# Moving a layer's activation tiles by some bytes in SBUF, and splitting its 512-column feed-forward products into 256-column ones

## The chip, the cores and the metric

The kernel runs on one core of one Trainium2 chip. TensorE multiplies 128x128 blocks into PSUM, VectorE (DVE) and ScalarE (ACT) work on SBUF and PSUM, GpSimd (POOL) and SyncE (SP) issue DMAs. The metric is the device time of one execution in microseconds; the time before is the median of three runs. SBUF has 128 partitions, and every tile begins at the same byte in each of them. That byte, modulo 256, is what this document calls a tile's start.

## The reference

One decoder layer on x of 256 tokens by 2048 channels, in float32:

```python
for l in range(DEPTH):                                  # DEPTH = 1
    mod = jax.nn.silu(c) @ w_ada[l] + b_ada[l]
    sh1, sc1, g1, sh2, sc2, g2 = jnp.split(mod[:, None, :], 6, axis=-1)
    h = x * (1.0 + sc1) + sh1
    y = token_mixer(h, ...)          # w_in, two mixers, two projections, w_out
    x = layer_norm(DEEPNORM_ALPHA * x + g1 * y, ln1_g[l], ln1_b[l])
    h = x * (1.0 + sc2) + sh2
    gate, up = jnp.split(h @ w_ffn_in[l], 2, axis=-1)   # 2048 x 11264
    y = (jax.nn.silu(gate) * up) @ w_ffn_out[l]         # 5632 x 2048
    x = layer_norm(DEEPNORM_ALPHA * x + g2 * y, ln2_g[l], ln2_b[l])
```

The token mixer projects h to queries, keys, values and gates, runs causal attention with 8 heads and a gated delta rule with 16 heads, projects both back to 2048 channels, merges them by sigmoid gates and projects once more.

## The kernel before, in words

**Products in parts.** TensorE multiplies in the fp32r type. To keep float32's accuracy each operand is split into a high part (rounded to fp32r) and a low part (the rest), and a product of two matrices is made of three: high by high, high by low, low by high. `split_w` (lines 221 and 222) splits every weight block of 128x1024 elements, the high part by an ACT copy and the low part by a DVE subtraction. `load_w` brings the block from HBM by a DMA on SP's queue; five raw blocks, four high and four low ones are held.

**Two ways to put a block through TensorE.** In `ws_mm` (lines 304 to 306) the weight is the stationary operand, 128x128 at a time, and the activations move: each product streams 256 columns, the 256 tokens, into one half of a PSUM bank. A block holds 4 contraction tiles by 2 output tiles, so it takes 8 times 3, or 24 products. Lines 304, 305 and 306 are high weight by high activation, high by low, low by high. Almost all of the input projection, the sigmoid gates and both projections back run this way. In `xs_unit` (lines 352 to 354) the activations are stationary and the weights move, 512 columns at a time: the attention's values, the delta rule's z, the output projection and the feed-forward output.

**The feed-forward input** has a third way, `ws_wide` (lines 309 to 316). There the high and the low part of an activation tile lie side by side in `h2`, so that one product of 512 columns (line 311) does high by high and high by low at once, into the two halves of a whole bank; after eight of these come eight products of 256 columns for the low weights (line 315), into the first half. That is 16 products a block. A unit is 256 columns of `w_ffn_in`, four blocks, and takes two banks of the four that `mm()` gives. When a unit is done, `summed` (lines 1222 to 1227) adds the two halves of each bank: an ACT copy and a DVE addition for each of two banks. Then come Silu for a gate unit, and for an up unit the product with the gate and the split for the next stage. The first two gate and two up units (line 1246 on) are made with `ws_mm` while the norm before them ends; the other 20 pairs, 40 units or 160 blocks, with `wide_unit`.

**Order of the work.** `step` and `run` put all blocks of the layer in one list; weights are loaded and split up to three blocks ahead. `tick` after each block lets side jobs advance: the delta rule and the attention, which are chains over DVE, ACT, PE and DMA (lanes "pre", "main", "moba"), and the sums over `w_ada` (line 241). Before the first weight blocks the kernel makes the first part of `mod`, and during the first 290 us it keeps loading 1 MB pieces of `w_ada` into the tiles of `ring`.

**Where the tiles lie.** A pool gives its tiles addresses in the order of their first use, after 4,096 bytes of scratch and four small constants. In bytes modulo 256 the tiles start as follows in the program before:

| tile | used as | start before |
|---|---|---|
| s0, s1 (h high, low; later the two halves of h2) | moving in lines 304 to 306, 311, 315; stationary in lines 352 to 354 for values and z | 128 |
| ya (attention's output) | moving | 128 |
| ybA, ybBh (delta rule's output) | moving | 64 |
| ybBl (delta rule's output, low, second half) | moving | 96 |
| weight blocks hi, lo | stationary in lines 304 to 315, moving in lines 352 to 354 | 64 |
| mh, ml, ach, acl | stationary in lines 352 to 354 | 64 |

Inside a tile every operand begins a multiple of 512 bytes further on.

Of the kernel before, what the change touches and what calls it, by code (L numbers as in the profile page):

```python
# [10 lines left out]
F32 = mybir.dt.float32  # L11
F32R = mybir.dt.float32r
AF = mybir.ActivationFunctionType
OP = mybir.AluOpType
# [4 lines left out]
P = 128  # L19
D = 2048  # L20
S = 256
KT = D // P
DFF = 5632
# [69 lines left out]
def layer(ctx, tc, a, out):  # L93
    nc = tc.nc
    v_, s_, g_, t_, dma = nc.vector, nc.scalar, nc.gpsimd, nc.tensor, nc.sync
    sdma = nc.gpsimd

    perm = ctx.enter_context(tc.tile_pool(name="perm", bufs=1))
# [10 lines left out]
    k1 = p1.enter_context(tc.tile_pool(name="p1", bufs=1))  # L109

    def e2(nm, shape):
        return k1.tile(shape, F32, tag="e2", name=nm, bufs=3)

    x_sb = perm.tile([P, KT, S], F32, tag="s2", name="x_sb")
    xv = a["x"][0].rearrange("(h p) d -> p h d", p=P)
    cols = perm.tile([P, V_END], F32, name="cols")
# [56 lines left out]
    def rest(n=1):  # L173
        return -n
# [52 lines left out]
    def split(hi, lo, src, scale=None):  # L227
        if scale is None:
            s_.copy(hi, src)
            v_.tensor_tensor(lo, src, hi.bitcast(F32), op=OP.subtract)  # L230
        else:
            s_.activation(hi, src, AF.Copy, scale=scale)
            v_.scalar_tensor_tensor(lo, src, scale, hi.bitcast(F32), op0=OP.mult, op1=OP.subtract)
# [39 lines left out]
    def mm():  # L273
        return pm.tile([P, 512], F32, tag="mm", name="mm")
# [3 lines left out]
    def step(w, k0, kn, c0, cn, post, begun=0, pin=False):  # L278
        prog.append((lambda: split_w(load_w(w, k0, kn, c0, cn), kn, cn, pin), post, begun))
# [25 lines left out]
                t_.matmul(o, hi[:, i, c], al, start=False, stop=False)  # L305
                t_.matmul(o, lo[:, i, c], ah, start=False, stop=(last and i == kn - 1 and t == 1))  # L306

    def ws_wide(box, both, hi, lo, k0, kn, first, last):
        for i in range(kn):
            for t in range(2):  # L310
                t_.matmul(box[t].rearrange("p (u i) -> p u i", u=2), hi[:, i, t * P:(t + 1) * P], both[k0 + i],  # L311
                          start=(first and i == 0), stop=False)
        for i in range(kn):
            for t in range(2):
                t_.matmul(box[t][:, :S], lo[:, i, t * P:(t + 1) * P], both[k0 + i][:, 0, :], start=False,  # L315
                          stop=(last and i == kn - 1))

    def pairs_of(ps):
        return ps.rearrange("p (t i) -> p t i", t=2)
# [85 lines left out]
    def g8(slot, nm, shape, dt=F32):  # L405
        return k1.tile(shape, dt, tag=f"g{slot}", name=nm)
# [9 lines left out]
    def load_ba():  # L416
# [1 line left out]

    kqs = [g8(2 * b, f"kq{b}", [P, 8, S]) for b in range(2)]
    vts = [g8(2 * b + 1, f"v{b}", [P, 8, S]) for b in range(2)]  # L420
    ring = [k1.tile([P, 2, 2048], F32, tag="ma0", name="r0"), k1.tile([P, 1, 2048], F32, tag="ma1", name="r1"),
            k1.tile([P, 1, 2048], F32, tag="g4", name="r2")]
    spare = ring[1][:, 0, :]
    ring = [t[:, i, :] for t in ring for i in range(t.shape[1])]
    jobs = []
# [121 lines left out]
    btd = dr.tile([VH, S], F32, name="btd")  # L547

    def gates_ba():
        w6 = k1.tile([P, 6, 2, VH], F32, name="w6")  # L550
        x, m, e, q, y, z = [w6[:, i] for i in range(6)]

        def heads(i):
            return dtb[:, i:i + 1, :].to_broadcast([P, 2, VH])

        tri = e2("tri", [P, 2, P])
        sdma.dma_start(tri, a["cst"][:, C_TRI:].rearrange("p (u i) -> p u i", u=2))
        ps = pg.tile([P, 2, 32], F32, tag="gd", name="ps_g")
        for i in range(2):
            t_.matmul(ps[:, i, :], ba[:, i * P:(i + 1) * P], cst[:, C_BA:C_BA + 32], start=True, stop=True)  # L560
        s_.activation(e, ps[:, :, 0:16], AF.Exp, scale=-1.0)
        v_.tensor_scalar(e, e, 1.0, None, op0=OP.add)
        v_.reciprocal(bcs[:, 3:5, :], e)
        v_.tensor_tensor(x, ps[:, :, 16:32], heads(0), op=OP.add)
        v_.tensor_scalar(m, x, -1.0, None, op0=OP.mult)
        v_.tensor_tensor(m, m, x, op=OP.max)
        s_.activation(e, m, AF.Exp, scale=-1.0)
        s_.activation(z, heads(1), AF.Exp)
        v_.tensor_scalar(q, e, 2.0, None, op0=OP.add)
        v_.reciprocal(q, q)  # L570
        v_.tensor_tensor(e, e, q, op=OP.mult)
        v_.tensor_tensor(q, e, e, op=OP.mult)
        v_.tensor_scalar(m, q, 1.0 / 15, None, op0=OP.mult)
        yield 1.2
        for n in (13, 11, 9, 7, 5, 3):
            v_.scalar_tensor_tensor(m, m, 1.0 / n, q, op0=OP.add, op1=OP.mult)
        v_.scalar_tensor_tensor(m, m, 1.0, e, op0=OP.add, op1=OP.mult)
        v_.tensor_scalar(x, x, 0.0, None, op0=OP.max)
        v_.scalar_tensor_tensor(x, m, 2.0, x, op0=OP.mult, op1=OP.add)
        v_.scalar_tensor_tensor(y, x, -1.0, z, op0=OP.mult, op1=OP.mult)  # L580
        yield 1.0
        yield rest()
        ps = pg.tile([P, 3, VH], F32, tag="gd", name="ps_c")
        t_.matmul(ps[:, 0:2, :], tri[:, 0, :], y, start=True, stop=True)
        t_.matmul(ps[:, 2, :], tri[:, 1, :], y[:, 0, :], start=True, stop=True)
        v_.tensor_copy(bcs[:, 0:3, :], ps)
        yield rest()
        tp = pt.tile([P, P], F32, tag="tp", name="tp")
        t_.transpose(tp[:80], bcs.rearrange("p u h -> p (u h)"), ident)
        rw = e2("gr", [80, P])  # L590
        s_.copy(rw, tp[:80])
        for i in range(2):
            c = slice(i * P, (i + 1) * P)
            sdma.dma_start(gcd[:, c], rw[16 * i:16 * i + 16])
            sdma.dma_start(btd[:, c], rw[48 + 16 * i:64 + 16 * i])
        yield 0.1
# [34 lines left out]
    def bc_heads(t, h0):  # L631
        return bass.AP(tensor=t.tensor, offset=t.offset + h0 * S, ap=[[0, P], [S, 2], [1, S]])

    kqn = [k1.tile([P, 3, 16], F32, name=f"kqn{b}") for b in range(2)]

    def squares(b, t0):
        ss = pg.tile([P, 512], F32, tag="gd", name="ss")
# [309 lines left out]
    cur = {}  # L947
# [80 lines left out]
    for j in range(8):  # L1028
        ws_unit(h_ops, w_in, O_GB + 256 * j, KT,
                lambda ps, j=j: s_.activation(cur["sgb"][:, 2 * j:2 * j + 2, :], ps, AF.Sigmoid))  # L1030
# [53 lines left out]
    def resid(ps, c0, cn, gb, base, dst, st, n):  # L1084
        cc = slice(c0, c0 + cn)
        for h in range(2):
            t = (cur["k3"].tile([P, 512], F32, tag="up", name="rt", bufs=2) if "k3" in cur
                 else e2("rt", [P, 512]))[:, :cn]
            v_.tensor_tensor(t, ps[h], gb[:, cc], op=OP.mult)
            v_.scalar_tensor_tensor(dst[:, h, cc], base[:, h, :], ALPHA, t, op0=OP.mult, op1=OP.add)  # L1090
            v_.bn_stats(st[:, h, n, :], dst[:, h, cc])
# [13 lines left out]
    def load_sqrt():  # L1105
        tc.keep_in_program_order(s_.activation(sm[:, 0, 0:1], epsc[:, 0:1], AF.Sqrt))

    sa = perm.tile([P, 2, KT], F32, name="sa")

    def mod2():  # L1110
        drain("ada")
        v_.tensor_scalar(sa[:, 0, :], adac[:, 64:80], 1.0, None, op0=OP.add)
        v_.tensor_tensor(sa[:, 1, :], sa[:, 0, :], cols[:, 112:128], op=OP.mult)
        v_.tensor_tensor(sa[:, 1, :], sa[:, 1, :], adac[:, 48:64], op=OP.add)
        v_.tensor_tensor(sa[:, 0, :], sa[:, 0, :], cols[:, 96:112], op=OP.mult)
        load_sqrt()
# [47 lines left out]
    h2_ops, act_ops = [[], []], [[], []]  # L1164
    pss, h2 = [], []
# [46 lines left out]
    def k3_tile(nm):  # L1212
        return cur["k3"].tile([P, 2, S], F32, tag=nm, name=nm, bufs=2)
# [5 lines left out]
        v_.tensor_tensor(sg, psu, sg, op=OP.mult)  # L1219
        split(ach[:, 2 * j:2 * j + 2, :], acl[:, 2 * j:2 * j + 2, :], sg)  # L1220

    def summed(box, nm):
        t = k3_tile(nm)
        for n in range(2):
            s_.copy(t[:, n, :], box[n][:, S:])
            v_.tensor_tensor(t[:, n, :], t[:, n, :], box[n][:, :S], op=OP.add)
        return t

    def wide_unit(c0, fin):
        box = []  # L1230
        for k in range(0, KT, 4):
            def post(hi, lo, k=k):
                if k == 0:
                    box.extend([mm(), mm()])
                ws_wide(box, h2, hi, lo, k, 4, k == 0, k == KT - 4)
                if k == KT - 4:
                    fin(box)
                tick()

            step(w_fi, k, 4, c0, 256, post)  # L1240
# [47 lines left out]
    do(ffn_more)  # L1288

    def ffn_unit(j):  # L1290
        def gate(box):
            sg = cur["sgw"] = summed(box, "sg")
            s_.activation(sg, sg, AF.Silu)

        def up(box):
            ach, acl = cur["act"]
            t = summed(box, "up")
            v_.tensor_tensor(t, t, cur["sgw"], op=OP.mult)
            split(ach[:, 2 * j:2 * j + 2, :], acl[:, 2 * j:2 * j + 2, :], t)

        wide_unit(256 * j, gate)
        wide_unit(DFF + 256 * j, up)

    for j in range(2, DFF // 256):
        ffn_unit(j)
# [76 lines left out]
    for n, (c0, cn) in enumerate(ln_blocks()):  # L1382
# [6 lines left out]
        def fin(ps, n=n, c0=c0, cn=cn):  # L1389
            cc = slice(c0, c0 + cn)  # L1390
            r = cur["r"]
            resid(ps, c0, cn, cur["g2b"], r[:, :, cc], r, cur["st"], n)
            for h in range(2):
                v_.tensor_tensor(r[:, h, cc], r[:, h, cc], cur["g"][:, cc], op=OP.mult)
# [41 lines left out]
```

## Time and profile before

| | us |
|---|---|
| median of 3 runs | 1731.93 |
| lowest, highest | 1727.89, 1731.94 |
| profiled execution, its own time | 1724.92 |
| span of its core | 1723.2 |
| PE busy | 1674.6 (97%) |
| DVE busy | 1232.4 (72%) |
| ACT busy | 819.3 (48%) |
| feed-forward input, wide part | 1028 to 1469 |

PE's granted clock was 1.00 of full speed in nearly all windows. Matmuls overlap: a product of 256 columns is shown as 0.28 us long, but the next one starts 0.11 to 0.12 us after it. So the price of a product is read from the distance between starts, in the timeline, and not from the mean of one. In the timeline, products of one line that follow each other directly are merged to one row with their count.

### The profile page before, as it was taken

What the parts mean: (1) busy time and instruction counts of PE and PEld (TensorE: products, weight loads), DVE (VectorE), ACT (ScalarE), POOL (GpSimd) and SP (SyncE); (2) the same over time, 40 slices, a digit from 0 to 9 for tenths busy, and PEclk for the clock granted to TensorE, in tenths of its full rate; (3) what the DMA queues carried; (4) which work ended last, traced back from release to release, by engine and by line L of the source; (5) the groups of instructions that cost most, each with busy time, mean ns of one, the idle gap of its engine ahead of it and who ended that gap; (6) DMA issues with size and microseconds to landing.
All of it is one profiled execution on the core that took longest, in us unless ns stands there. A gap on an engine that the chain in (4) does not pass through costs nothing.

```text
span 1723.2 us, 28196 instructions
## 1 busy us (share of the span) xinstructions
PE 1674.6 (97%) x11129; PEld 1518.9 (88%) x11129; DVE 1232.4 (72%) x1775; ACT 819.3 (48%) x1134; POOL 39.5 (2%) x61
## 2 busy tenths in 40 slices
PE   6999999999999998999989999999999999999998
PEld 4898999889999777999978998888888888888898
DVE  6899987899755796567986787666666655455454
ACT  3544445868545445464334454444444444433342
POOL 0000010110100001000000000000000000000000
PEclk9999999999999999999999999999999999999999
DMA  9999996665777668678998468777777756755652
GB/s 365 335 363 348 338 328 218 186 205 167 244 235 231 209 214 266 218 225 262 306 347 288 159 206 271 240 237 241 231 246 231 241 190 194 236 196 183 202 189 98
DMA packets 114296, 417.43 MB, mean 242 GB/s; under 512 B 13406, under 2 KB 14414, under 8 KB 108656
## 3 DMA queue, kind: packets, MB, share of 16 engines
q1 hardware_dynamic: 109652, 400.12, 69.3%
q0 software_dynamic: 4512, 15.51, 3.3%
q8 instruction: 87, 1.43, 0.3%
q14 instruction: 45, 0.37, 0.1%
HBM read 408.14 MB, written 7.44 MB: 241 GB/s over the span
## 4 chain that ended last, share of the span: by engine, by line
PE 76%; DVE 8%; issue 7%; DMA 6%; ACT 1%; POOL 0%; SPq 0%; DVEq 0%; ACTq 0%; POOLq 0%
PE mm L311 17%; PE mm L315 9%; PE mm L306 8%; PE mm L304 8%; PE mm L305 8%; PE mm L353 6%; PE mm L354 6%; PE mm L352 6%; DVE lo L222 3%; DMA raw_a<-in_w_ada 2%; DVE r L241 1%; PE ps L757 1%; ACT hi L221 1%; DMA mbd<-ma 1%; PE mm L370 1%
## 5 line engine op out<-in xcount | busy, mean ns | idle before, releaser
L221 ACT CAST hi<-raw 128x1024 fp32r<-128x1024 f32 (+2 forms) x572 | 581.3, 1020 | 769.2 <-PE mm L311 199.1
L222 DVE TENSOR_TENSOR lo<-raw,hi 128x1024 fp32r<-128x1024 f32 (+2 forms) x572 | 672.2, 1185 | 278.1 <-ACT hi L221 275.1
L304 PE MATMUL mm<-s,hi 128*128 128x256 f32 x1184 | 338.1, 286 | 5.3 <-ACT hi L221 5.0
L306 PE MATMUL mm<-s,lo 128*128 128x256 f32 x1184 | 333.0, 282 | 8.1 <-DVE lo L222 7.9
L305 PE MATMUL mm<-s,hi 128*128 128x256 f32 x1184 | 332.5, 281 | 0.0
L311 PE MATMUL mm<-h,hi 128*128 128x512 f32 x1280 | 319.0, 391 | 0.0
L311 PEld LDWEIGHTS mm<-h,hi 128*128 128x128 f32 x1280 | 228.8, 188 | 39.5
L304 PEld LDWEIGHTS mm<-s,hi 128*128 128x128 f32 x1184 | 224.9, 190 | 10.3 <-ACT hi L221 8.0
L306 PEld LDWEIGHTS mm<-s,lo 128*128 128x128 f32 x1184 | 223.6, 189 | 11.2 <-DVE lo L222 10.2
L305 PEld LDWEIGHTS mm<-s,hi 128*128 128x128 f32 x1184 | 224.7, 190 | 0.3
L315 PEld LDWEIGHTS mm<-h,lo 128*128 128x128 f32 x1280 | 171.1, 188 | 13.2
L315 PE MATMUL mm<-h,lo 128*128 128x256 f32 x1280 | 174.1, 278 | 0.0
L353 PE MATMUL mm<-lo,ach 128*128 128x512 f32 (+1 forms) x352 | 127.7, 363 | 0.0
L352 PE MATMUL mm<-hi,ach 128*128 128x512 f32 (+1 forms) x352 | 127.7, 363 | 0.0
L354 PE MATMUL mm<-hi,acl 128*128 128x512 f32 (+1 forms) x352 | 127.6, 363 | 0.0
L241 DVE CUSTOM_DVE_ANT_0 raw_a<-raw_a,cb,cols 128x1024 f32<-128x1024 f32 x56 | 71.9, 1283 | 76.6 <-DMA raw_a<-in_w_ada 76.5
L241 DVE CUSTOM_DVE_ANT_0 raw_a<-raw_a,cb,ada_half 128x1024 f32<-128x1024 f32 x56 | 71.9, 1283 | 62.1 <-DMA raw_a<-in_w_ada 62.1
L241 DVE CUSTOM_DVE_ANT_0 r<-r,cb,cols 128x2048 f32<-128x2048 f32 (+1 forms) x40 | 92.6, 2322 | 8.5 <-DMA r<-in_w_ada 8.4
L353 PE MATMUL mm<-lo,s 128*128 128x512 f32 x192 | 76.7, 399 | 3.2 <-DVE lo L222 3.1
L352 PE MATMUL mm<-hi,s 128*128 128x512 f32 x192 | 77.3, 404 | 0.0
L354 PE MATMUL mm<-hi,s 128*128 128x512 f32 x192 | 75.9, 395 | 0.0
L353 PEld LDWEIGHTS mm<-lo,ach 128*128 128x128 f32 x352 | 66.5, 189 | 10.6 <-DVE lo L222 0.2
(342 smaller groups left out, 2435.7 us busy)
## 6 DMA issues: line engine op xcount, KB each, us to landing
raw<-in_w_ffn_in SPq DMA_DIRECT2D x176, 512.0 KB, 4.4
raw<-in_w_in SPq DMA_DIRECT2D x168, 512.0 KB, 4.6
raw_a<-in_w_ada SPq DMA_DIRECT2D x112, 512.0 KB, 4.5
raw<-in_w_ffn_out SPq DMA_DIRECT2D x88, 512.0 KB, 4.0
r<-in_w_ada SPq DMA_DIRECT2D x40, 1024.0 KB, 8.2
raw<-in_w_proj_gdn SPq DMA_DIRECT2D x32, 512.0 KB, 4.9
raw<-in_w_out SPq DMA_DIRECT2D x32, 512.0 KB, 5.0
raw<-in_w_in SPq DMA_DIRECT2D x40, 384.0 KB, 5.3
```

The source lines that it names most:

```text
L221: s_.copy(hi, raw)
L222: low = v_.tensor_tensor(lo, raw, hi.bitcast(F32), op=OP.subtract)
L241: v_.tensor_tensor_reduce(out=raw, in0=raw, in1=cb[:, n * part:n * part + n], scale=1.0, scalar=cols[:, col:col + 1] if first else h, op0= ...
L304: t_.matmul(o, hi[:, i, c], ah, start=(first and i == 0 and t == 0), stop=False)
L305: t_.matmul(o, hi[:, i, c], al, start=False, stop=False)
L306: t_.matmul(o, lo[:, i, c], ah, start=False, stop=(last and i == kn - 1 and t == 1))
L311: t_.matmul(box[t].rearrange("p (u i) -> p u i", u=2), hi[:, i, t * P:(t + 1) * P], both[k0 + i], start=(first and i == 0), stop=False)
L315: t_.matmul(box[t][:, :S], lo[:, i, t * P:(t + 1) * P], both[k0 + i][:, 0, :], start=False, stop=(last and i == kn - 1))
L352: t_.matmul(box[h], xh, hi[:, i, :], start=start, stop=False)
L353: t_.matmul(box[h], xh, lo[:, i, :], start=False, stop=False)
L354: t_.matmul(box[h], xl, hi[:, i, :], start=False, stop=stop)
L370: t_.matmul(box[h], xh, hi[:, i, :], start=k == 0, stop=False)
```

## The change

Four tiles are created at another place in the program, and two unused ones are added, so that the addresses of others shift; and `ws_wide`, `summed` and `wide_unit` are replaced by `ws_late` and `late_unit`.

- `sa` (128 bytes) is now the first tile of the pool `perm`. x_sb, ya, s0, s1 and what lies between move up by 128 bytes, to a start of 0. The weight blocks stay where they are.
- `kqn0` (192 bytes) is now in front of ma0, whose place ybA takes later, and ma1 (ybBh). Both go from 64 to 0. `space0` (64 bytes) keeps g4, which later holds a half of ml, at 64. `space1` (96 bytes) brings the tiles of tag m4, among them ybBl, from 96 to 0.
- In the feed-forward input a block takes 24 products of 256 columns. First come, for each of the 8 stationary tiles of the high weights, high by high and high by low into the same half of one bank; then the 8 products of the low weights. A unit takes one bank, and its sum is complete there: `summed` goes, and Silu and the product with the gate read PSUM.

The core of the diff:

```diff
+    sa = perm.tile([P, 2, KT], F32, name="sa")
     x_sb = perm.tile([P, KT, S], F32, tag="s2", name="x_sb")
...
-    def ws_wide(box, both, hi, lo, k0, kn, first, last):
+    def ws_late(ps, ops, hi, lo, k0, kn, first, last):
         for i in range(kn):
             for t in range(2):
-                t_.matmul(box[t].rearrange("p (u i) -> p u i", u=2), hi[:, i, t * P:(t + 1) * P], both[k0 + i],
-                          start=(first and i == 0), stop=False)
+                o, w = ps[:, t * S:(t + 1) * S], hi[:, i, t * P:(t + 1) * P]
+                t_.matmul(o, w, ops[0][k0 + i], start=(first and i == 0 and t == 0), stop=False)
+                t_.matmul(o, w, ops[1][k0 + i], start=False, stop=False)
         for i in range(kn):
             for t in range(2):
-                t_.matmul(box[t][:, :S], lo[:, i, t * P:(t + 1) * P], both[k0 + i][:, 0, :], start=False,
-                          stop=(last and i == kn - 1))
+                t_.matmul(ps[:, t * S:(t + 1) * S], lo[:, i, t * P:(t + 1) * P], ops[0][k0 + i], start=False,
+                          stop=(last and i == kn - 1 and t == 1))
...
-    ring = [k1.tile([P, 2, 2048], F32, tag="ma0", name="r0"), k1.tile([P, 1, 2048], F32, tag="ma1", name="r1"),
-            k1.tile([P, 1, 2048], F32, tag="g4", name="r2")]
+    kqn = [k1.tile([P, 3, 16], F32, name="kqn0")]
+    ring = [k1.tile([P, 2, 2048], F32, tag="ma0", name="r0"), k1.tile([P, 1, 2048], F32, tag="ma1", name="r1")]
+    k1.tile([P, 16], F32, name="space0")
+    ring.append(k1.tile([P, 1, 2048], F32, tag="g4", name="r2"))
...
     def gates_ba():
+        k1.tile([P, 24], F32, name="space1")
         w6 = k1.tile([P, 6, 2, VH], F32, name="w6")
...
-    kqn = [k1.tile([P, 3, 16], F32, name=f"kqn{b}") for b in range(2)]
+    kqn.append(k1.tile([P, 3, 16], F32, name="kqn1"))
...
-    def summed(box, nm):
-        t = k3_tile(nm)
-        for n in range(2):
-            s_.copy(t[:, n, :], box[n][:, S:])
-            v_.tensor_tensor(t[:, n, :], t[:, n, :], box[n][:, :S], op=OP.add)
-        return t
...
     def ffn_unit(j):
-        def gate(box):
-            sg = cur["sgw"] = summed(box, "sg")
-            s_.activation(sg, sg, AF.Silu)
+        def gate(ps):
+            cur["sgw"] = k3_tile("sg")
+            s_.activation(cur["sgw"], ps, AF.Silu)
...
-        def up(box):
+        def up(ps):
             ach, acl = cur["act"]
-            t = summed(box, "up")
-            v_.tensor_tensor(t, t, cur["sgw"], op=OP.mult)
-            split(ach[:, 2 * j:2 * j + 2, :], acl[:, 2 * j:2 * j + 2, :], t)
+            sg = cur["sgw"]
+            v_.tensor_tensor(sg, ps, sg, op=OP.mult)
+            split(ach[:, 2 * j:2 * j + 2, :], acl[:, 2 * j:2 * j + 2, :], sg)
```

More of the change, by code (lines that the diff above doesn't have):

```diff
@@ L1106, in load_sqrt @@
         tc.keep_in_program_order(s_.activation(sm[:, 0, 0:1], epsc[:, 0:1], AF.Sqrt))
-    sa = perm.tile([P, 2, KT], F32, name="sa")
     def mod2():
@@ L1220, in act, with late_unit @@
         split(ach[:, 2 * j:2 * j + 2, :], acl[:, 2 * j:2 * j + 2, :], sg)
-    def summed(box, nm):
-        t = k3_tile(nm)
-        for n in range(2):
-            s_.copy(t[:, n, :], box[n][:, S:])
-            v_.tensor_tensor(t[:, n, :], t[:, n, :], box[n][:, :S], op=OP.add)
-        return t
-    def wide_unit(c0, fin):
+    def late_unit(c0, fin):
         box = []
@@ L1233, in post @@
                 if k == 0:
-                    box.extend([mm(), mm()])
-                ws_wide(box, h2, hi, lo, k, 4, k == 0, k == KT - 4)
+                    box.append(mm())
+                ws_late(box[0], h2_ops, hi, lo, k, 4, k == 0, k == KT - 4)
                 if k == KT - 4:
-                    fin(box)
+                    fin(pairs_of(box[0]))
                 tick()
@@ L1290, in ffn_unit @@
     def ffn_unit(j):
-        def gate(box):
-            sg = cur["sgw"] = summed(box, "sg")
-            s_.activation(sg, sg, AF.Silu)
-        def up(box):
+        def gate(ps):
+            cur["sgw"] = k3_tile("sg")
+            s_.activation(cur["sgw"], ps, AF.Silu)
+        def up(ps):
             ach, acl = cur["act"]
-            t = summed(box, "up")
-            v_.tensor_tensor(t, t, cur["sgw"], op=OP.mult)
-            split(ach[:, 2 * j:2 * j + 2, :], acl[:, 2 * j:2 * j + 2, :], t)
-        wide_unit(256 * j, gate)
-        wide_unit(DFF + 256 * j, up)
+            sg = cur["sgw"]
+            v_.tensor_tensor(sg, ps, sg, op=OP.mult)
+            split(ach[:, 2 * j:2 * j + 2, :], acl[:, 2 * j:2 * j + 2, :], sg)
+        late_unit(256 * j, gate)
+        late_unit(DFF + 256 * j, up)
     for j in range(2, DFF // 256):
```

## The prediction

> **What bounds the kernel now.** I read the page's totals first, then busy time by stage, then the groups of products, then the timeline at the rate of single products.
>
> ```profile
> span 1723.2 us, 28196 instructions
> ...
> PE 1674.6 (97%) x11129; PEld 1518.9 (88%) x11129; DVE 1232.4 (72%) x1775; ACT 819.3 (48%) x1134; POOL 39.5 (2%) x61
> ```
>
> ```profile
> core 0: us, PE busy (x) PEld busy (x) DVE busy (x) ACT busy (x) POOL busy (x), PEclk, DMA share, GB/s
> 40.00:120.00 80.00, 75.15 (x607) 71.51 (x607) 72.27 (x91) 41.59 (x65) 0.00 (x0) 0.99 0.96 354
> 120.00:200.00 80.00, 76.11 (x617) 72.40 (x617) 76.10 (x89) 33.54 (x46) 0.00 (x0) 1.00 0.94 344
> 200.00:290.00 90.00, 90.00 (x767) 89.35 (x766) 76.30 (x98) 42.48 (x53) 5.24 (x9) 1.00 0.82 282
> ...
> 655.00:780.00 125.00, 117.25 (x986) 115.30 (x987) 76.23 (x127) 64.54 (x118) 4.65 (x5) 0.97 0.72 230
> 780.00:877.00 97.00, 96.92 (x807) 96.44 (x806) 82.02 (x108) 39.09 (x43) 0.00 (x0) 1.00 0.89 301
> ...
> 1028.00:1466.00 438.00, 438.00 (x2544) 385.69 (x2543) 289.57 (x350) 211.69 (x278) 0.00 (x0) 1.00 0.72 232
> ```
>
> TensorE is busy 97% of the span, and all of it from 1028 to 1466 us, the feed-forward input. There DVE works 289.6 of 438 us, and DMA has 28% to spare. Before 200 us PE has holes (75.15 of 80 us) and DMA stands at 0.94 to 0.96: there the weights arrive no faster than they are used. From 655 to 780 us PE has holes again, at the delta rule's chain; one row of the waits is 5.1 us:
>
> ```profile
> PE ps L757 <- DMA TT<-ubd: 5.1, 2, 4.3
> ```
>
> So time is won or lost through the distance between products' starts, wherever PE has no holes. How many products there are:
>
> ```profile
> L304 PE MATMUL mm<-s,hi 128*128 128x256 f32 x1184 | 338.1, 286 | 5.3 <-ACT hi L221 5.0
> L306 PE MATMUL mm<-s,lo 128*128 128x256 f32 x1184 | 333.0, 282 | 8.1 <-DVE lo L222 7.9
> L305 PE MATMUL mm<-s,hi 128*128 128x256 f32 x1184 | 332.5, 281 | 0.0
> L311 PE MATMUL mm<-h,hi 128*128 128x512 f32 x1280 | 319.0, 391 | 0.0
> ...
> L304 PE MATMUL mm<-ya,hi 128*128 128x256 f32 x128 | 36.4, 285 | 0.0
> L304 PE MATMUL mm<-ybA,hi 128*128 128x256 f32 x128 | 36.4, 284 | 0.0
> L305 PE MATMUL mm<-ybBl,hi 128*128 128x256 f32 x128 | 36.3, 284 | 0.0
> ...
> L304 PE MATMUL mm<-h,hi 128*128 128x256 f32 x112 | 31.2, 280 | 0.0
> L304 PE MATMUL mm_kept<-s,hi 128*128 128x256 f32 x96 | 27.0, 282 | 0.0
> ```
>
> Each kind has its other two lines with the same count. That gives 3 x 1184 + 3 x 96 = 3840 products with s0 and s1 moving, 384 with ya, 768 with ybA or ybB, 336 in the first feed-forward blocks. The 1280 of line 311 are 160 blocks. Now the distances, first where the activations move:
>
> ```profile
> 249.75 0.28 PE L306 MATMUL mm<-s,lo 128*128 128x256 f32 x1
> ...
> 250.81 0.28 PE L306 MATMUL mm<-s,lo 128*128 128x256 f32 x1
> ```
>
> ```profile
> 283.75 0.28 PE L306 MATMUL mm<-s,lo 128*128 128x256 f32 x1
> ...
> 284.77 0.28 PE L306 MATMUL mm<-s,lo 128*128 128x256 f32 x1
> ```
>
> ```profile
> 839.94 0.28 PE L306 MATMUL mm<-ybBh,lo 128*128 128x256 f32 x1
> ...
> 841.38 0.28 PE L306 MATMUL mm<-ybBh,lo 128*128 128x256 f32 x1
> ```
>
> ```profile
> 1500.48 0.39 PE L353 MATMUL mm<-lo,ach 128*128 128x512 f32 x1
> ...
> 1501.16 0.39 PE L353 MATMUL mm<-lo,ach 128*128 128x512 f32 x1
> ```
>
> From 249.75 to 250.81 lie 9 products, 117.8 ns each: a tile that starts at 128 modulo 256. From 283.75 to 284.77 lie 9 of the same kind, with the same tiles, at 113.3 ns. So at this start there are two rhythms, and PE can stay in either. From 839.94 to 841.38 lie 12 with the delta rule's output, which starts at 64 or 96, at 120.0 ns. The last fence has 3 products of 512 columns, with weights moving that start at 64: 226.7 ns each. At the same start 256 columns more cost 226.7 - 120.0 = 106.7 ns; that is the streaming, and the extra of a product is 13.3 ns at 64 whatever its length, and 6.7 or 11.1 ns at 128. The trace has no fp32r product whose moving operand starts at 0.
>
> The feed-forward blocks:
>
> ```profile
> 1201.37 2.00 PE L311 MATMUL mm<-h,hi 128*128 128x512 f32 x8
> 1203.20 1.07 PE L315 MATMUL mm<-h,lo 128*128 128x256 f32 x8
> 1204.11 1.99 PE L311 MATMUL mm<-h,hi 128*128 128x512 f32 x8
> 1205.93 1.11 PE L315 MATMUL mm<-h,lo 128*128 128x256 f32 x8
> 1206.88 2.00 PE L311 MATMUL mm<-h,hi 128*128 128x512 f32 x8
> ```
>
> Two blocks take 1206.88 - 1201.37 = 5.51 us, one 2.755 us: 1.83 us for eight of 512 columns (229 ns each) and 0.91 or 0.95 us for eight of 256.
>
> **The change part by part.** *The feed-forward input.* 160 blocks of 24 products replace 160 x 2.755 us. Break-even is at 2.755 / 24 = 114.8 ns a product. At 117.8 the stage loses 160 x (2.827 - 2.755) = 11.5 us, at 113.3 it gains 5.7 us.
>
> *What a start of 0 gives.* This cost the trace doesn't show. Bounds above: 120.0 ns, the worst start seen; 117.8 if nothing changes. Below: every product loads a new stationary block, and a row shows how fast that can go when the streaming is short:
>
> ```profile
> 751.88 1.05 PE L798 MATMUL pr<-vn,ma 128*128 128x128 f32 x8
> ```
>
> ```profile
> L798 PE MATMUL pr<-vn,ma 128*128 128x128 f32 x32 | 4.2, 274 | 0.0
> ```
>
> Eight products of 128 columns with a weight load each: (1.05 - 0.27) / 7 = 111 ns from start to start. I take this as the floor of a chain in which each product has its own load; the lowest value for 256 columns is 113.3. From 64 to 128 the extra fell from 13.3 to 11.1 or 6.7 ns, so at 0 I expect what is left of it to vanish or to leave the slow rhythm out. I take 112.2, the middle of 111 and 113.3, as nearest to the better rhythm that is already there; for the range, 109 (between the streaming of 106.7 and 111) and 120.
>
> The Trainium skill's page "TensorE: Matmul & The Clock Gate", section "Back-to-back issue gap", gives a warm gap of N / 2.4 + 2.5 ns, 109.2 ns for 256 and 215.8 for 512 columns, whatever the address. By it a block goes from 2.600 to 2.621 us, the change costs 3.3 us and the result is 1735 us; the distances above, 229 and 113.3 to 120, disagree with it.
>
> Sum for the stage at 112.2: 160 x (24 x 0.1122 - 2.755) = -9.9 us.
>
> *Other products whose moving tile shifts.* s0 and s1: 3840 x (117.8 - 112.2) = 21.5 us, less about 300 products that ran in the 113.3 rhythm already (1.4 us, an estimate from the stretches around 30, 80 and 280 us): 20.1. ya: 384 x 5.6 = 2.2. ybA and ybB: 768 x 7.8 = 6.0. First feed-forward blocks, about half of which ran at 113.3 (an estimate from the timeline, where the rhythm changes at 1011 us): 336 x 3.5 = 1.2. Together 29.5 us of PE time. Not all of it counts. Before 200 us lie 607 + 617 products; at DMA shares of 0.96 and 0.94 the weights can come only some 5% faster, so I take half of their 6.9 us: -3.4. From 655 to 780 us the delta rule's chain waits for DMAs and DVE, not for PE; of that stage's 4.5 us (some 800 products) I take half: -2.2. That leaves 23.9 us.
>
> *s0 and s1 as stationary operand* (values and z, 576 products of 512 columns) go from 128 to 0 too:
>
> ```profile
> 581.79 0.39 PE L353 MATMUL mm<-lo,s 128*128 128x512 f32 x1
> ...
> 582.49 0.39 PE L353 MATMUL mm<-lo,s 128*128 128x512 f32 x1
> ```
>
> Three products take 0.70 us with s (233 ns), against 0.68 us with ach above, which starts at 64 (226.7 ns). Bounds: 576 x 6.7 = 3.9 us either way; I take 2 us of gain.
>
> *Evictions.* The 80 ACT copies and 80 DVE additions of `summed` go:
>
> ```profile
> L1225 ACT COPY sg<-mm 128x256 f32<-128x256 f32 x40 | 12.8, 371 | 0.0
> L1226 DVE TENSOR_TENSOR sg<-sg,mm 128x256 f32<-128x256 f32 x40 | 14.9, 414 | 0.0
> ```
>
> 80 x 0.37 = 30 us of ACT and 80 x 0.41 = 33 us of DVE, both beside a PE that never waits in this window: nothing. A unit holds one bank instead of two, so a bank is free earlier: nothing too. The last unit's chain gets shorter, but its output is used only at the end of a 22-block unit. If PE became fast enough to feel it, DVE's 66% would fall to 59%: the cover grows. No DMA or wait is added, and none of the moved tiles carries another instruction.
>
> Sum: -9.9 - 23.9 - 2 = -35.8 us. The profiled execution took 1724.92 us (span 1723.2 and 1.7 around it), so it would be 1689; the median of the runs lies 7.0 us above it, 1731.93 - 35.8 = **1696 us**.
>
> **The rivals.**
>
> *The start doesn't matter below 128, and the 256-column products cost more than the wide ones* (slower). The extra belongs to each product, not to the address; 24 products of 117.8 replace 8 of 229 and 8 of 116, everything else stays. +11.5 us in the feed-forward input, -1.7 where 64 becomes 128-like: 1742 us. It decides from 114.8 ns upwards in that stage, from about 116 for the sum. For it: PE ran at 117.8 for most of the span, and went to 113.3 at the same addresses, so something other than the start picks the rhythm. Against: 64 and 128 differ. The Trainium skill's page "SBUF — State Buffer", section "Specifications (TRN2)", counts lines of 16 bytes; by it all starts here are alike and this rival would hold; the 120.0 against 117.8 and 113.3 speaks against that page's figure as the whole story. The rule on the gap above is of the same kind, an extra for each product whatever its address, at a smaller price. 17%.
>
> *A start of 0 collides with weights at 64.* The 512-column products are at 226.7 where both operands start at 64, at 229 with moving 128 and stationary 64, and at 233 with moving 64 and stationary 128. If the difference of the two counts, 0 against 64 may be as bad as 120 ns: +20 us in the feed-forward input, 3840 x 2.2 + 1.4 + 384 x 2.2 + 336 x 4.3 = 12 us elsewhere, 1764 us. 6%.
>
> *PE gets faster and only the feed-forward input shows it.* DMA and DVE take the place of PE before 290 us, the delta rule's chain to 780. Left are 9.9, the 7 of ybA, ybB and the first blocks, and 2: 1713 us. For it: the holes in three of the stages above. Against: 200 to 290 us is full at a DMA share of 0.82. 11%.
>
> *PE falls from one rhythm to the other as now.* At 0 there are still both, 113.3 and 117.8 in one part to two, mean 116.3 ns: feed-forward +5.8 us, elsewhere -7: 1731 us, no change. 6%.
>
> **How the numbers follow.** The forecast, products at 109 to 113.3 ns, has 60%. Its own ends: at 113.3 the gains are 5.7 and 19 us, 1707; at 109, 22, 37 and 3.9 us, 1669. A measurement of this kernel tells about 0.3%, 5 us, from no change. Faster: the forecast and the third rival, 71%; same: the fourth, 6%; slower: the first two, 23%. The range runs from 1667, a little below the better end, to 1744, so that the first rival is in and the second is out.
>
> **What would show it.** In the timeline of the feed-forward input, 24 products a block, with starts 111 to 113.3 ns apart and a block at 2.66 to 2.72 us; over 2.755 the step is wrong. The same distance from 200 to 290 us with s, and where 120 stood with ybA and ybB. Before 200 us DMA at 0.97 or more; the L757 wait longer than 5.1 us. No rows of L1225 and L1226. If all distances stay at 117.8, or if both rhythms alternate, my reading of the start is wrong.

## The result and the profile after

The changed kernel takes 1720.94 us (median of 22 runs, 1705.68 to 1733.66), the kernel before, on the same chips, 1731.63 us (22 runs, 1722.53 to 1738.93). The ratio is 0.9933, with a 95% interval of 0.9914 to 0.9953: faster by 0.7%, under a third of what was forecast. The ratios leave out the runs counted as slow: here four, from 1732.08 to 1733.66 us, whose granted clock (0.990 to 0.992) is that of the others and with which the ratio of the means is 0.995, and with the weights at 128 (below) one of 2352.58 us at a clock of 0.655.

The profiled execution of the changed kernel took 1726.41 us, which is 1.5 us more than that of before. From the page after, the totals and the three groups of the feed-forward input that stand where line 311 and line 315 stood:

```profile
span 1724.6 us, 30521 instructions
...
PE 1675.8 (97%) x12409; PEld 1571.8 (91%) x12409; DVE 1204.2 (70%) x1695; ACT 796.9 (46%) x1054; POOL 39.5 (2%) x61
...
L314 PE MATMUL mm<-h,hi 128*128 128x256 f32 x1280 | 308.8, 281 | 0.0
L313 PE MATMUL mm<-h,hi 128*128 128x256 f32 x1280 | 308.7, 281 | 0.0
...
L317 PE MATMUL mm<-h,lo 128*128 128x256 f32 x1280 | 176.8, 281 | 0.0
```

PE is as busy as before, with 1280 products more. Where the time went is seen from two instants. The view of one line gives how many instructions it has, the shortest, middle and longest time that one is shown with (in ns), and when the first and the last of them start. For line 311 before, and for line 313 after, that is the stretch of the 160 blocks; for line 352 (354 after) with s, the first start is the end of the startup. (The count behind the shape at the end of a row is not used here.)

```profile
L311 PE MATMUL mm<-h,hi x1280: 388/392/394, 1027.7 to 1467.6; 128*128 128x512 f32 x183
L352 PE MATMUL mm<-hi,s x192: 392/394/588, 299.3 to 658.5; 128*128 128x512 f32 x192
```

```profile
L313 PE MATMUL mm<-h,hi x1280: 281/281/281, 1017.9 to 1469.0; 128*128 128x256 f32 x183
L354 PE MATMUL mm<-hi,s x192: 388/388/628, 294.0 to 651.9; 128*128 128x512 f32 x192
```

The startup ends 5.3 us earlier (294.0 against 299.3), the stretch from there to the first block (1017.9 less 294.0) is 4.5 us shorter (723.9 against 728.4), and the blocks take 451.1 us from first to last, against 439.9: 11.2 us more. So ahead of the feed-forward input there is a gain of 9.8 us, and in it a loss that takes back more than all of it. The timeline shows why, with two neighbouring groups of eight low-weight products, one block apart:

```profile
1200.66 1.10 PE L317 MATMUL mm<-h,lo 128*128 128x256 f32 x8
...
1203.48 1.10 PE L317 MATMUL mm<-h,lo 128*128 128x256 f32 x8
```

A block takes 2.82 us; from the whole stretch, 451.1 us for 3830 distances between starts (159 blocks and 14 products of the last), a product takes 117.8 ns. The long rhythm, which the prediction gave up at a start of 0, held for all 3840 products of this execution. With s, in contrast, the products from 203 to 274 us ran at 113.3 ns where before they ran at 117.8. The table by stage and two rows of PE's waits, the same windows and columns as before:

```profile
40.00:120.00 80.00, 74.74 (x617) 70.88 (x616) 73.09 (x92) 40.98 (x63) 0.00 (x0) 1.00 0.95 360
120.00:200.00 80.00, 75.35 (x623) 71.42 (x622) 76.46 (x91) 34.24 (x46) 0.00 (x0) 1.00 0.95 347
200.00:290.00 90.00, 90.00 (x792) 89.36 (x791) 78.16 (x104) 43.85 (x55) 5.24 (x9) 1.00 0.83 291
...
655.00:780.00 125.00, 121.35 (x1060) 120.12 (x1059) 78.75 (x119) 63.99 (x117) 2.65 (x3) 0.99 0.73 244
780.00:877.00 97.00, 94.49 (x759) 89.77 (x758) 85.37 (x114) 38.19 (x41) 1.10 (x2) 1.00 0.90 314
```

```profile
PE mm L307 <- DVE lo L223: 9.3, 12, 2.3
...
PE ps L762 <- DVE kqn L653: 3.8, 1, 3.8
```

Where PE has no holes, from 200 to 290 us, 792 products fit instead of 767. Before 200 us the holes are a little larger (74.74 and 75.35 us busy) at DMA shares of 0.95. From 780 to 877 us, where PE was busy 96.92 of 97 us, it now is 94.49, with DMA at 314 instead of 301 GB/s. The window doesn't hold the same work, though: the projection of the delta rule's output now ends at 864.4 us, where it ended at 878.4. Of the 2.5 us of holes 1.5 lie behind 864.4, in the output projection, whose first 13.6 us had 1.3 us of holes before; 1.0 us is new, nearly all of it a wait for low weights. The waits of products for the low weights rose from 7.9 to 9.3 us over the span. The delta rule's wait for a DMA, 5.1 us before, is not in this list, and one for DVE has 3.8 where it had 0.6; but the second execution of the same program (below) has both, 5.3 and 3.3 us, so these two differ from execution to execution and show nothing of the change.

### The profile page after: what moved, and what is told of

The parts are those of the page before. It is cut to its first block, busy times and chain, and to the rows that moved or that the text cites. A ratio compares the mean times of both kernels' runs of the same rounds, so it can differ in the third digit from the quotient of the medians.

```text
span 1724.6 us, 30521 instructions
## 1 busy us (share of the span) xinstructions
PE 1675.8 (97%) x12409; PEld 1571.8 (91%) x12409; DVE 1204.2 (70%) x1695; ACT 796.9 (46%) x1054; POOL 39.5 (2%) x61
## 4 chain that ended last, share of the span: by engine, by line
PE 79%; DVE 9%; DMA 7%; issue 3%; ACT 2%; SPq 0%; POOL 0%; DVEq 0%; ACTq 0%; POOLq 0%
PE mm L314 9%; PE mm L313 9%; PE mm L317 9%; PE mm L307 8%; PE mm L305 8%; PE mm L306 8%; PE mm L355 6%; PE mm L356 6%; PE mm L354 6%; DVE lo L223 4%; DMA raw_a<-in_w_ada 3%; DVE r L242 1%; DMA raw<-in_w_proj_gdn 1%; PE ps L762 1%; ACT hi L222 1%
## 5 line engine op out<-in xcount | busy, mean ns | idle before, releaser
L314 PE MATMUL mm<-h,hi 128*128 128x256 f32 x1280 | 308.8, 281 | 0.0
L313 PE MATMUL mm<-h,hi 128*128 128x256 f32 x1280 | 308.7, 281 | 0.0
L313 PEld LDWEIGHTS mm<-h,hi 128*128 128x128 f32 x1280 | 242.3, 189 | 0.0
L314 PEld LDWEIGHTS mm<-h,hi 128*128 128x128 f32 x1280 | 241.6, 189 | 0.0
L307 PEld LDWEIGHTS mm<-s,lo 128*128 128x128 f32 x1184 | 225.5, 191 | 11.9 <-DVE lo L223 10.7
L317 PEld LDWEIGHTS mm<-h,lo 128*128 128x128 f32 x1280 | 162.5, 189 | 0.0
L354 PE MATMUL mm<-hi,s 128*128 128x512 f32 x192 | 76.9, 402 | 0.0
```

The lines of the kernel that those rows point to most:

```text
L313: t_.matmul(o, w, ops[0][k0 + i], start=(first and i == 0 and t == 0), stop=False)
L314: t_.matmul(o, w, ops[1][k0 + i], start=False, stop=False)
L317: t_.matmul(ps[:, t * S:(t + 1) * S], lo[:, i, t * P:(t + 1) * P], ops[0][k0 + i], start=False, stop=(last and i == kn - 1 and t == 1))
L354: t_.matmul(box[h], xh, hi[:, i, :], start=start, stop=False)
```

## The experiments

Four theories stood at first. A: a product takes 113.3 or 117.8 ns, which of them is settled when PE starts again after an interruption (another kind of product, a wait), and is kept until the next one. B: the order of products in `ws_late` makes the 117.8. C and D: only chance, or only the evictions. Later came F (the distance between the two operands' starts counts), G and H (what eats the gain ahead of the feed-forward input). Distances are the moving start minus the stationary one, modulo 256: 64 for s and h2 before, 192 after, 0 for ybA before.

**The same kernel again.** No edit.

> The changed kernel once more, unchanged, one more execution to look into. Theory A (rhythm kept from the last restart): a product of 256 columns takes 113.3 or 117.8 ns; which of the two is settled whenever PE starts again after an interruption, and is then kept. The 160 blocks of the feed-forward input have no interruption, so all of them, 3840 products, are in one rhythm: 452 us in one execution and 435 us in another. If this execution fell on the other side, the stage shows 113.3 ns; if on the same, 117.8 again. Rival B (the order of the products, three into one half bank, makes the 117.8): 117.8 ns in every execution.

The view of line 313 in this execution:

```profile
L313 PE MATMUL mm<-h,hi x1280: 275/276/277, 1020.8 to 1454.8; 128*128 128x256 f32 x183
```

The stretch takes 434.0 us, 17 less than in the first execution of the same program, and its neighbouring blocks are 2.72 us apart, which is 24 products at 113.3 ns. The run took 1712.25 us. B is out: the order of products is the same in both. That one program has two times, 17 us apart, in its longest stage also accounts for much of the 28 us over which its runs spread; not for all, since the runs of the kernel before spread over 16 us.

**The starts alone.** `sa`, `kqn0`, `space0` and `space1` as in the change, `ws_wide`, `wide_unit` and `summed` as before.

> The starts moved to 0, the feed-forward input with 512-column products as before. Theory A: the products with s, ya, ybA and ybB mostly at 113.3 ns, as in the changed kernel, and the feed-forward input at or a little under its 441 us: some 15 to 20 us faster than before, about 1714. Rival C (the gain outside the feed-forward input in the profiled execution was chance): within 5 us of before.

1720.8 us, ratio 0.9961 (0.9939 to 0.9983): half of what A expected, and more than C allowed, so chance alone is out. In the profiled execution the first block begins at 1020.3 us, 7.4 earlier than before, and the blocks take 442.6 us from first to last, 2.7 longer. A stretch of its feed-forward timeline:

```profile
1203.37 2.02 PE L312 MATMUL mm<-h,hi 128*128 128x512 f32 x8
1205.24 1.07 PE L316 MATMUL mm<-h,lo 128*128 128x256 f32 x8
1206.15 2.02 PE L312 MATMUL mm<-h,hi 128*128 128x512 f32 x8
1208.01 1.07 PE L316 MATMUL mm<-h,lo 128*128 128x256 f32 x8
1208.92 2.02 PE L312 MATMUL mm<-h,hi 128*128 128x512 f32 x8
```

Two blocks take 5.55 us, against 5.51 before. All low-weight groups have the short rhythm now (1.07), but the 512-column groups before them last 1.87 instead of 1.83 us: a product of 512 columns got longer at distance 192, about 233 against 229 ns.

**The 256-column products alone.** `ws_late` and `late_unit` as in the change, all starts as before.

> The feed-forward input with 256-column products, the starts left at 128, 64 and 96. Theory A: at 128 a restart lands in the long rhythm about nine times in ten, so the stage takes 452 us in nearly all executions and the rest stays as before: 9 to 12 us slower, about 1742. Rival B: the same 452 us; it differs from A only with the starts at 0. Rival D (the products alone save time by the PSUM reads and DVE work that go): within 3 us of before.

1740.72 us, ratio 1.007 (1.0051 to 1.009), slower as A said; D is out.

```profile
L312 PE MATMUL mm<-h,hi x1280: 279/279/280, 1032.4 to 1483.5; 128*128 128x256 f32 x183
```

451.1 us: at distance 64 the blocks are in the long rhythm. (The first block starts at 1032.4 us here and at 1027.7 in the kernel before, with the same program up to there: single executions differ by that much.) One half of the change gains 0.4%, the other loses 0.7%, and both together gain 0.7%. The parts can't be added: the 256-column products pay only where the short rhythm can be had, and the starts decide how often that is.

**One more product a unit.**

```diff
+                if k == 0:
+                    t_.matmul(cur["other"], hi[:, 0, :P], h2_ops[0][0][:, :P], start=True, stop=True)
                 ws_late(box[0], h2_ops, hi, lo, k, 4, k == 0, k == KT - 4)
```

> The changed kernel with one more product of 128 columns into an unused bank at the beginning of each of the 40 units of the feed-forward input (some 0.1 to 0.2 us each, 4 to 8 us in all; its result is used nowhere). Theory A: each is an interruption after which the rhythm is settled anew, so units of both rhythms stand side by side, about two of three at 113.3 ns; mean about 114.8, stage 441 us and 4 to 8 for the added products. Rival B: all units at 117.8, 452 us and 4 to 8.

1726.86 us, ratio 0.9982 (0.9963 to 1.0). The rhythm is settled anew, but not at random, and half of the units are short, not two of three. Three of the added products:

```profile
1191.36 0.22 PE L1232 MATMUL other<-h,hi 128*128 128x128 f32 x1
...
1202.38 0.22 PE L1232 MATMUL other<-h,hi 128*128 128x128 f32 x1
...
1213.80 0.22 PE L1232 MATMUL other<-h,hi 128*128 128x128 f32 x1
```

From one to the next lie 11.02 and then 11.42 us, 96 products and the added one each: one unit at 113.3, the next at 117.8 (4.5 ns times 96 is 0.4 us), and so on through all 40. An added product of 128 columns turns the rhythm over each time.

**Five lengths of the added product.** As before, with `n = (32, 64, 96, 160, 192)[unit // 8]` columns.

> As the run with one added product a unit, but of 32 columns in the first eight units, then 64, 96, 160 and 192 in eight each; a look at the rhythms, not at the time. Theory A: the added product shifts the phase in which the next ones start, and the shift depends on its length. With 128 columns each unit went over to the other rhythm. At least one length should keep the rhythm of the unit before, or lead to 113.3 ns from both. If every length turns it over, the number of products and not their length counts.

With 32, 64, 96 and 160 columns, units at 113.3 ns came singly, after two or three at 117.8. With 192 the short rhythm stayed:

```profile
1384.32 0.25 PE L1234 MATMUL other<-h,hi 128*128 128x192 f32 x1
...
1395.74 0.25 PE L1234 MATMUL other<-h,hi 128*128 128x192 f32 x1
...
1406.75 0.25 PE L1234 MATMUL other<-h,hi 128*128 128x192 f32 x1
```

The unit from 1384.32 took 11.42 us, the next 11.01, and those after it 10.99 each. The same added product after a long unit led now to a long and now to a short one, in a nearly regular turn. That fits a phase which each added product shifts by an amount that depends on its length; the phase itself no run shows. (The run took 1729.02 us.)

**192 columns in the first six units.**

```diff
+                if k == 0 and cur["unit"] < 6:
+                    cur["unit"] += 1
+                    t_.matmul(cur["other"], hi[:, 0, :P], h2_ops[0][0][:, :192], start=True, stop=True)
```

> The changed kernel with an added product of 192 columns at the beginning of the first six units of the feed-forward input alone (result used nowhere). In the run with five lengths, 192 columns led from the long rhythm to the short one within two units and then kept it. Theory A: from the fourth or so unit on all products at 113.3 ns in every execution, the stage at 435 to 440 us instead of 435 or 452; median about 1712, and a smaller spread than the changed kernel's 1705.7 to 1733.7. Rival (what 192 did was chance): units at 117.8 remain, median 1720 as the changed kernel.

1714.31 us, ratio 0.9923 (0.99 to 0.9945).

```profile
L313 PE MATMUL mm<-h,hi x1280: 276/276/303, 1021.4 to 1456.0; 128*128 128x256 f32 x183
```

434.6 us, every unit in the short rhythm, and six times between 1712.74 and 1716.67. In the profiled execution the stage was in the short rhythm from its first unit, so that this execution shows only that 192 columns keep it; the narrow spread of six runs speaks for their leading to it, but doesn't show it.

**All starts at 0.** 192 bytes ahead of the weight tiles; distance 0.

> The changed kernel with 192 bytes put ahead of the weight tiles, so that these too start at 0 (ybBl alone at 32). Theory A as it stands says nothing of the weights' start. If the two rhythms come from the distance between the moving and the stationary start (0 against 64 now), equal starts leave one rhythm, as 64 against 64 did with 120.0 ns at all times; then the 256-column products are all at one value. If the moving start alone counts, nothing changes with s: 113.3 and 117.8 side by side, and the values, z and feed-forward output, whose moving weights go from 64 to 0, get shorter than 226.7 ns or show two rhythms. Rival E (no start matters below 16 bytes): as the changed kernel, 1710 to 1728 us.

1752.22 us, ratio 1.0139 (1.0111 to 1.0166).

```profile
L313 PE MATMUL mm<-h,hi x1280: 283/283/283, 1035.1 to 1494.7; 128*128 128x256 f32 x183
```

459.6 us, 120.0 ns a product, and 120.0 ns with s too: the value that ybA had before, where both operands started at 64. A moving start of 0 gains nothing by itself, and rival E falls. The products of 512 columns with s now lie at distance 0 and come down to about 227 ns.

**Weights at 128.** 64 bytes ahead of the weight tiles; distance 128.

> The changed kernel with the weight tiles at 128 and the activations at 0, a distance between moving and stationary start of 128; so far there were 0 (120.0 ns at all times), 64 and 192 modulo 256 (both rhythms). Theory F (the distance between the two starts counts): a rhythm of its own, other than the mix at 64 and 192. If the distance counts modulo 128, 120.0 ns as at 0, feed-forward stage 461 us. If the moving start alone counts, as the changed kernel: 435 or 452 us.

1746.51 us (middle one of three runs), ratio 1.0103 (1.007 to 1.0136).

```profile
L313 PE MATMUL mm<-h,hi x1280: 279/281/285, 1029.6 to 1484.1; 128*128 128x256 f32 x183
```

454.5 us, 118.7 ns a product on average, and about the same with s. That is neither the 120.0 of distance 0 nor one of the two rhythms: it isn't the distance modulo 128 that counts, and neither of the expectation's two alternatives to F holds.

**Both moved by 64.** The moving activations at 64, the weights at 128, six products of 192 columns as above; distance 192 again.

> As the run with 192 added columns in the first six units, but all activations that move start at 64 (ybBl at 160) and the weights at 128: other starts, the same distance of 192 modulo 256 as 0 against 64. Theory F (the distance between moving and stationary start counts, not the moving start): the same rhythms as there, the feed-forward units at 435 to 436 us with 113.3 ns a product, median 1714 within 5 us. Theory I (a moving start of 0 modulo 256 is what makes 113.3 likely): a start of 64 gives 120 ns at all times as ybA did, units at 461 us, about 1750.

1716.45 us, ratio 0.994 (0.9917 to 0.9964), four times between 1714.67 and 1719.43.

```profile
L314 PE MATMUL mm<-h,hi x1280: 276/276/303, 1022.5 to 1457.2; 128*128 128x256 f32 x183
```

434.7 us. At a moving start of 64 the short rhythm is there as at 0, once the weights are moved along. Theory I falls, F stands. The edit also puts 256 bytes more between the activations and the weights, and the rhythm is the same, which fits a distance that counts modulo 256.

**The changed kernel beside it.**

> The changed kernel unchanged, beside the shifted pair on one chip, for its spread and a third execution to look into. Theory A: the feed-forward units at 435 or 452 us in this execution, and times spread over 15 us or more, while the shifted pair's, whose rhythm is led to the short one, lie within 6 us. Rival B: 452 us and no wider spread than the other.

1713.35 us, ratio 0.9926 (0.9899 to 0.9952), seven times between 1707.92 and 1727.73; the profiled one, the third execution here, had its blocks in 434.0 us, so B is out once more. The spread is 20 us, against 5 us of the shifted pair, as A said. In the median it isn't slower than the versions with added products: these make the time steadier, and no version was shown to beat the changed kernel's median.

**Without most loads of w_ada**, in the changed kernel and in the kernel before:

```diff
-                dma.dma_start(raw, w_ada.tile(8 * half, 8, col * P, P, by_column=True))
+                src = w_ada.tile(8 * half, 8, col * P, P, by_column=True)
+                if load:
+                    dma.dma_start(raw, src)
```

> The changed kernel without the loads of w_ada between the startup and the feed-forward input: the sums on DVE stay but read another tile, so the sums are not those of the reference, and some 36 MB of loads are left out. Beside it the same of the kernel before. Theory G (ahead of the feed-forward input PE's gain is lost to weights that arrive late): without these loads the stretch from the startup's end to the feed-forward input is shorter by 12 us or more than in the kernel before with the same loads left out. Rival H (lost to the delta rule's chain over DVE, which these loads don't touch): the difference stays at the 3 to 6 us that the two full kernels show.

> The kernel before without the same loads of w_ada (DVE's sums stay and read another tile). Theory G: ahead of the feed-forward input at most 5 us shorter than the full kernel before, since PE is the bound there at 117.8 and 120.0 ns a product. Rival H: the same here; it differs in the kernel beside it.

The views of the feed-forward's high products and of the first values' products, in the changed kernel without the loads and in the kernel before without them:

```profile
L315 PE MATMUL mm<-h,hi x1280: 276/276/276, 994.8 to 1428.9; 128*128 128x256 f32 x183
L356 PE MATMUL mm<-hi,s x192: 388/391/586, 294.9 to 640.5; 128*128 128x512 f32 x192
```

```profile
L313 PE MATMUL mm<-h,hi x1280: 388/392/397, 1009.8 to 1449.8; 128*128 128x512 f32 x183
L354 PE MATMUL mm<-hi,s x192: 392/394/587, 298.5 to 648.5; 128*128 128x512 f32 x192
```

From the startup's end to the first feed-forward block the changed kernel needs 699.9 us and the kernel before 711.3, so the gain is 11.4 us. With the loads it was 4.5 us in the first execution (723.9 against 728.4), 0.5 us in the second (292.9 to 1020.8 is 727.9) and 1.9 us in the third. G's 12 us are missed by 0.6, H's 3 to 6 by 5. (What was left out are 80 loads of 512 KB, 42 MB and not 36.) These are single executions, of 1686.34 and 1707.01 us without the loads, and with them the stretch differs: the run with the 256-column products alone, which has the starts of the kernel before, needs 734.5 us there. So a part of the gain is lost to the loads, but how large a part is open.

The stages show it more clearly. From the first product with ybA to the first with mh the kernel before takes 93.9 us without the loads and the changed kernel 88.9. With the loads it is 94.6 us before (93.9 in the run with the 256-column products alone), and 92.6, 94.2 and 94.4 in the three executions of the changed kernel. In the output projection behind it (first product with mh to first with h) no start differs; without the loads it takes 93.3 us in both kernels, with them 99.4 and 100.8 at the starts of before and 101.2 to 103.4 after. PE's waits for split weights, from 290 us to the feed-forward blocks, are 10.7 to 12.6 us in the changed kernel and 0.7 without the loads. G's other expectation failed: without the loads the kernel before, too, is 17.1 us shorter here, not 5 at most. It already waited for weights, 8.9 us, which come down to 0.2. The waits of the delta rule's products into ps (line 757 before) lie between 4.5 and 10.0 us with the loads and are 4.3 and 4.8 without; they differ too much between executions to say what the chain adds.

## Why the prediction came out as it did

The direction was right, and 1720.94 us lies inside 1667 to 1744, but the forecast gain of 35.8 us was more than three times the measured 10.7. That the direction came out is luck: with the same starts of 0 for the activations, but the weights at 0 too, the kernel is slower by 1.4%. The gain hangs on where the weights happened to lie, and of the forecast's terms none asked for that.

- **The price of a product at a start of 0** is the step that failed: "so at 0 I expect what is left of it to vanish or to leave the slow rhythm out. I take 112.2". No stretch is below 113.3 ns in any run, and the long rhythm is not left out: ahead of the feed-forward input the products with s that follow each other without a gap take 114.7 ns on average in the first execution, against 117.3 before. The fourth rival, both rhythms as now, was the right mechanism, at 6%. Its mix was not: counted from all starts in the traces (stretches of at least six 256-column products, ahead of the feed-forward blocks), 8 of 88 stretches at distance 64 had the short rhythm before, and 69 of 102 at distance 192 after.
- **The feed-forward term** was -9.9 us. It is +11.2 or -5.9, by execution, since 3840 products without interruption take the one or the other. I had the two values, +11.5 and -5.7, almost to the point, and then took one price for all executions that is better than both. Of four profiled executions of this stage without added products three were short; a stage without interruption is never at the mean.
- **The terms ahead of it**, -23.9 and -2, came to -9.8, -6.9 (second execution: first block at 1020.8 against 1027.7) and -6.6 in the third. The term of 2 us held: with s as the stationary operand 512 columns take 229 ns instead of 233, 2.3 us for 576 products. But some of the other products stayed at 117.8; and the third rival, loads and chain in place of PE, is in good part true: I discounted the time before 200 and from 655 to 780 us, but not 780 to 975. DMA's share stood at 0.89 there from 780 to 877 before, and of the 6.0 us forecast for ybA and ybB at most 2.0 came with the loads, and 5.0 without them.
- **The variable was wrong.** The start of the moving operand alone doesn't set the price: at 0 it is 120.0, 118.7, or 113.3 and 117.8 ns, by the weights' start. The second rival looked at the right one, the distance to the stationary start, but read its sign from products of 512 columns: at 192 these are the slowest (233 ns) and those of 256 columns the fastest.
- **The floor of 111 ns** from weight loads was never reached and wasn't tested. The gap of 109.2 ns for 256 columns by the Trainium skill ("TensorE: Matmul & The Clock Gate", "Back-to-back issue gap"), whose formula that section gives for a product by itself, appears in no run for these products; the formula has no term for the address, and the runs have 113.3 to 120.0 ns by address. The 16-byte lines of the Trainium skill ("SBUF — State Buffer", "Specifications (TRN2)") don't tell apart starts that are all multiples of 32, and the runs do.
- **Evictions** gave nothing, as said: line 1225's copies are gone, and PE is busy all 438.00 us from 1028 to 1466 us in both; what follows, from the first product with ach (1468.8 to 1723.2 before, 1470.2 to 1724.6 after), takes 254.4 us in both.

What lies behind the two rhythms, why a distance of 192 favours the short one, and what adds 6.7 ns at a distance of 0, no run shows.

## What to carry to other kernels

Read the distance between starts of products and not their busy time, and look for two values of the same product in one trace: where there are two, the next execution may draw the other, so one profile doesn't price an edit. Place stationary and moving tiles with regard to each other, and measure the distance for the product's own length. In a kernel whose engines are all near their limits, ask of each microsecond saved on PE whether the next weights are there.

## What the runs showed of the hardware

Starts of fp32r products, 128x128 stationary, one weight load each, by the distance of the moving from the stationary start modulo 256 bytes:

| distance | 256 columns, ns | 512 columns, ns |
|---|---|---|
| 0 | 120.0 at all times | 226.7 |
| 64 | 117.8, seldom 113.3 | 229 |
| 128 | 118.7 on average | 232 (with s, a wider scatter) |
| 192 | 113.3 or 117.8, kept until an interruption | 233 |

At 192 an added product of 128 columns turned the rhythm over 39 times in succession, and one of 192 columns kept the short one each time.
